# Three kinds of work at the end of a ConvFFN, moved one or two steps later

## The chip, the cores and the metric

The kernel runs on one core of a Trainium2 chip. The metric is the time of one launch in device microseconds. Before the change it is 2572.07 us, the median of three runs (2570.33 to 2573.21). The core has five engines that run side by side, each working through its own queue in order: TensorE (PE in the profile; its weight loads are PEld), VectorE (DVE), ScalarE (ACT), GpSimd (POOL) and SyncE (SP), which here only issues DMA transfers. Some transfers are issued from POOL's queue, those that add into DRAM.

## The reference

The program is a trunk of two layers over 1024 rows of width 1024 in float32: layer 0 has a gated DeltaNet and a ConvFFN, layer 1 a chunked attention and a ConvFFN, each with an RMSNorm ahead and a residual sum behind, and a final RMSNorm. The change concerns the ConvFFN, which both layers have, and what follows it in layer 0:

```python
def rmsnorm(x, g):
    xf = x.astype(jnp.float32)
    y = xf * lax.rsqrt(jnp.mean(xf * xf, axis=-1, keepdims=True) + EPS)
    return (y * g.astype(jnp.float32)).astype(x.dtype)

def conv_ffn(xn, w_up, conv_w, conv_b, w_down):
    h = causal_dwconv(xn @ w_up, conv_w) + conv_b          # 3 taps along the rows
    gate, val = h[..., :FFN_DIM], h[..., FFN_DIM:]         # FFN_DIM = 2816 = 22 tiles of 128
    return (jax.nn.silu(gate) * val) @ w_down
...
        h = h + conv_ffn(rmsnorm(h, f_norm[layer]), f_w_up[layer], f_conv[layer], f_conv_b[layer], f_w_down[layer])
```

## The kernel before

Every matrix product is done in float32 by three matmuls of rounded parts: an operand is rounded to `fp32r` (the high part, a copy on ScalarE), the rest is a difference (the low part, a subtraction on VectorE or GpSimd), and high by high, low by high and high by low are summed in PSUM. A "rounding" is that pair of instructions: `uh`/`ul` for the first weights, `dh`/`dl` and `eh`/`el` for the second product, `hidh`/`hidl` for hidden tiles, `fh`/`fl` for the last weights.

`ffn` (line 1423, called once for each layer) goes through 22 tiles j of 128 hidden channels. A tile has a gate half and a value half of 128 x 1024. The two products with the first weights are done by a scheme with seven block products instead of eight (`product`, in the order n = 1, 7, 6, 5, 2, 4, 3), whose banks are read and combined by `after`: ScalarE copies `keep` (n = 1) and half of `gpre` (n = 2); VectorE makes two `keep` sums (n = 6), the halves of `vpre` (n = 5 and 4) and the other half of `gpre` (n = 3). Product 4 adds into the bank of product 7, which the second `keep` sum reads first. Then a tile is convolved: `taps` (line 1544) makes step 0 on ScalarE (L1553) and steps 1 and 2 on VectorE (L1556), for value and gate; `silu` (L1559) is on ScalarE; `gated` (line 1561) multiplies value by gate on VectorE; `hidden` (line 1564) rounds the result. There is one buffer for `gate`.

The first 18 tiles go through a second scheme in pairs (`second`, `drain`, `send`), which ends in DMA sums into DRAM. The last four tiles, 18 to 21, are multiplied directly with the last rows of the second weights into banks `pf`: in layer 0 by `part` (eight output tiles m, three passes over them for the first 512 rows: tiles 18 and 19, then 20, then 21; then one pass for the other 512 rows), in layer 1 by `tile_of`, the same with eight row tiles. The last weights are loaded by `load_last`, and `cut_last` (line 1855) rounds them: q is the output tile in layer 0; the low part is VectorE's for even q and GpSimd's for odd q. Tile 21, the last, is convolved in halves of 512 rows: `half(c0, c1)` (line 1712) returns two functions, the first with the three value taps and the first two gate taps, the second with the last gate tap, `silu`, `gated` and `hidden`.

The order is written by hand. `step(key, f)` appends a step of matmuls to a list `seq` and notes its place in `pos`; `at(i, f, rank)` books other work ahead of step i. At the end one loop (line 1992 on) goes through the steps: for each it sorts the booked work by rank (equal ranks keep the order of booking), issues it, and then issues the step. All five engines get their instructions in that order:

```python
            for i in range(len(seq) + 8):
                for _, f in sorted(jobs.pop(i, ()), key=lambda j_: j_[0]):
                    f()
                if i < len(seq):
                    seq[i]()
```

`end` is the place of tile 21's last product (n = 3), `fin_at` that of the second scheme's last product; `nx(j, s)` is the place of product number s of the next tile, and for the last tile `end + s`. `pf` of output tile 0 is step `end + 1`, of output tile 1 `end + 2`, and so on.

Behind layer 0's `ffn` stands the norm of its result (`norm_steps`, line 391). `closing` (line 1884) adds `pf` to the residual `h` on VectorE, and with each `h` goes a square on ScalarE (`nacc` for the first, `nt` for the others, L399) and a sum on VectorE (L401); the last sum is L409. For the first 512 rows the column sums `pss` (L412) and the spread `psb` (L425) are matmuls among those of the second pass. While that runs, `load_w` and `split_w` (line 91) load and prepare the attention's first weights: a load into `wraw`, a fold with a norm's gains on ScalarE (L96, eight small instructions), `whi` on ScalarE (L102) and `wlo` on GpSimd (L104). This work is outside the hand-written list: its place among the norm's instructions on ScalarE and SP is chosen by the Tile framework's own ordering.

Of the kernel before, what the change touches and what calls it, by code (L numbers as in the profile page):

```python
# [19 lines left out]
HALF = 512  # L20
NH_A = 8
NH_B = 16
FP = 22
# [5 lines left out]
def trunk_kernel(  # L29
# [541 lines left out]
    with ExitStack() as ph:  # L571
# [140 lines left out]
        def heads(t):  # L712

            return t // 2, range(4 * (t % 2), 4 * (t % 2) + 4)
# [656 lines left out]
        with tc.manual_schedule(engines={mybir.EngineType.PE, mybir.EngineType.DVE, mybir.EngineType.Activation}):  # L1371
            tails = []
            acts, normed = [[[[None, None] for _ in range(KT)] for _ in range(2)] for _ in range(2)]
            for t in range(4):
                s, hds = heads(t)
# [47 lines left out]
    def ffn(layer, h, hp, xs, tail, d_r, last):  # L1423
# [19 lines left out]
        def at(i, f, rank=1):  # L1443

            jobs.setdefault(max(i, 0), []).append((rank, f))
# [98 lines left out]
        def taps(j, v, step, c0=0, c1=SEQ):  # L1544
            w, m = cf[:, layer, FP * v + j, :], FP * v + j
            if (j, v) not in conv_t:
                if v == 0:
                    conv_t[j, v] = tp.tile([P, SEQ], F32, name="gate", tag="gate")
                else:
                    conv_t[j, v] = hp.tile([P, SEQ], F32, name="val", tag=f"h{layer + 1}_{j % 4}")  # L1550
            t_, p_ = conv_t[j, v], pre[j, v]
            if step == 0:
                nc.scalar.activation(t_[:, c0:c1], p_[:, c0:c1], AF.Identity, scale=w[:, 2:3], bias=cfb[:, layer, m : m + 1])  # L1553
            else:
                a = max(c0, step)
                nc.vector.scalar_tensor_tensor(t_[:, a:c1], p_[:, a - step : c1 - step], w[:, 2 - step : 3 - step], t_[:, a:c1], op0=ALU.mult, op1=ALU.add)  # L1556

        def silu(j, c0=0, c1=SEQ):
            nc.scalar.activation(conv_t[j, 0][:, c0:c1], conv_t[j, 0][:, c0:c1], AF.Silu)  # L1559

        def gated(j, c0=0, c1=SEQ):
            tt(nc.vector, conv_t[j, 1][:, c0:c1], conv_t[j, 1][:, c0:c1], conv_t[j, 0][:, c0:c1], ALU.mult)

        def hidden(j, c0=0, c1=SEQ):

            if j not in hid:
                if j == FP - 1:
                    hid[j] = [fin.tile([P, SEQ], F32R, name=f"hid{i}", tag=f"hid{i}") for i in "hl"]
                else:
                    room_ = {18: (5, 6), 19: (7, 2), 20: (3, 4)}[j]  # L1570
                    hid[j] = [hp.tile([P, SEQ], F32R, name=f"hid{i}", tag=f"h{layer + 1}_{n}") for n, i in zip(room_, "hl")]
            (hh, hl), v_ = hid[j], conv_t[j, 1]
            nc.scalar.copy(hh[:, c0:c1], v_[:, c0:c1])
            tt(nc.vector, hl[:, c0:c1], v_[:, c0:c1], hh[:, c0:c1].bitcast(F32), sub)
# [29 lines left out]
        pos = {}  # L1604
# [42 lines left out]
        end, fin_at = pos[FP - 1, 7], pos["d", NG - 1, 4]  # L1647
# [15 lines left out]
        def nx(j, s):  # L1663
            return pos[j + 1, s] if j + 1 < FP else end + s
# [24 lines left out]
        for j in range(3, FP - 1):  # L1689
# [3 lines left out]
        v0, v1, v2, g0, g1, g2 = [(v, i) for v in (1, 0) for i in range(3)]  # L1693
        when = {
            0: [(11, (g0,), 0), (12, (v0,), 0), (13, (v1,), 2), (13, (v2,), 2.7), (15, (g1, g2, silu), 2), (17, (gated,), 2)],
            1: [(18, (v0, v1), 2), (19, (v2, g0), 2), (20, (g1,), 2), (21, (g2, silu), 2), (22, (gated,), 2)],
            2: [(24, (v0, v1), 2), (25, (v2, g0), 2), (26, (g1,), 2), (27, (g2, silu), 2), (28, (gated,), 2)],
        }
        for j in range(3, FP - 1):
            late_ = 1 if j == FP - 2 else 0  # L1700
            when[j] = [(pos[j, 7], (v0, v1), 2), (nx(j, 1), (v2, g0), 2), (nx(j, 2 + late_), (g1,), 2)]
            when[j] += [(nx(j, 3 + late_), (g2,), 2), (nx(j, 4 + late_), (silu,), 1.6), (nx(j, 5 + late_), (gated,), 2)]
            if j >= 2 * NG:
                when[j].append(({18: fin_at + 5, 19: pos[FP - 1, 5], 20: end + 1}[j], (hidden,), 1.9))
        for j, w_ in when.items():
            for i, fs, r in w_:
                at(i, lambda j=j, fs=fs: [taps(j, *f) if isinstance(f, tuple) else f(j) for f in fs], r)
# [4 lines left out]
        def half(c0, c1):  # L1712
            return (
                lambda: (taps(FP - 1, 1, 0, c0, c1), taps(FP - 1, 1, 1, c0, c1), taps(FP - 1, 1, 2, c0, c1), taps(FP - 1, 0, 0, c0, c1), taps(FP - 1, 0, 1, c0, c1)),
                lambda: (taps(FP - 1, 0, 2, c0, c1), silu(FP - 1, c0, c1), gated(FP - 1, c0, c1), hidden(FP - 1, c0, c1)),
            )
# [5 lines left out]

        fin = None
        at(end, open_fin, -2)
        at(end, half(0, HALF)[0], 2)
        at(end + 1, half(0, HALF)[1], 2)
        at(end + 2, lambda: (half(HALF, SEQ)[0](), half(HALF, SEQ)[1]()), 2)

# [108 lines left out]
        fw, fh, fps, norms = {}, {}, {}, []  # L1837
        n0 = len(seq)
        slots = [(k, 1) for k in range(4)] + [(k, 1) for k in range(4, 8)] if layer == 0 else [(k, 0) for k in range(4)] + [(k, 1) for k in range(4)]
        last_at = [pos[FP - 1, s] for s in (3, 4, 5, 6)] + ([end, end, end + 1, end + 1], [end + 1, end + 1, end + 3, end + 3])[layer]  # L1840

        def load_last(q):
            tag = ("a11", "a12", "r11", "r21", "r22", "r11", "r22", "r21")[q]
# [18 lines left out]
        for q in range(8):  # L1862
            s = (1, 1, 2, 3, 4, 4, 5, 6)[q]
# [143 lines left out]
    d_h = [dram.tile([P, SEQ], F32, name=f"d_h{k}") for k in range(KT)]  # L2007
    xb = ([[None, None] for _ in range(KT)], [[None, None] for _ in range(KT)])
    ctx_f, tail0 = ffn(0, h, hp, normed, tails[0], d_r0, xb)
    ctx_o = ctx.enter_context(ExitStack())  # L2010
    wp = ctx_o.enter_context(tc.tile_pool(name="wp1", bufs=2, **SB))
# [315 lines left out]
    def norm_out(t, ht, fin):  # L2327
# [34 lines left out]
        return go()  # L2362

    ctx_f, _ = ffn(1, h, hp, normed, tails[0], d_r1, norm_out)
    ctx_f.close()
    ctx_h.close()
# [56 lines left out]
```

## Time and profile before

| | before |
|---|---|
| median of the runs | 2572.07 us |
| profiled execution, its own time | 2572.95 us |
| its span | 2571.2 us |
| TensorE busy | 2504.6 us (97%) |
| VectorE, ScalarE, GpSimd busy | 72%, 55%, 57% |
| tile 21's products and `pf` in layer 0 | about 1260 to 1334 us of the span |
| the same in layer 1 | about 2492 to 2565 us |

The span is the time from the first to the last instruction in the profile; the execution's own time is 1.75 us longer. A row of a timeline has the start in the span, the duration, the engine, the line and operation, the tile written and the tiles read, and a count; in brackets stands how long the engine was idle before it and what ended that. Rows that follow each other without idle time and have the same line are merged. A window's row has the busy time of each engine (with the number of instructions), then the granted TensorE clock as a share of full speed, the DMA share and GB/s. A row of the waits has the total, the count and the longest, in microseconds. Most of the helper functions record under one line, so L1428 is every elementwise operation of `ffn` and L1449 every rounding's copy but those of `cut_last` (L1858) and `hidden` (L1573).

### The profile page before, as it was taken

To read this page: it belongs to the slowest core of one execution; us is meant where nothing else is said; L and a number is where in the kernel's file an instruction comes from. 1 tells how busy PE (TensorE), PEld (TensorE's weight loads), DVE (VectorE), ACT (ScalarE), POOL (GpSimd) and SP (SyncE) were. 2 spreads that over 40 slices of the span, in tenths; PEclk is the share of its full clock that TensorE was granted. 3 is DMA by queue.
4 is the path that set the end of the run, shared out by engine and by line. 5 is a ranking of instruction groups with operands and counts; after the bars stand their busy time and mean duration, and the time that the engine had idled before them with its cause. 6 is when DMAs were issued, how large, how long until landed. Compare 5 with 4: busy or idle time off the path is not lost.

```text
span 2571.2 us, 39377 instructions
## 1 busy us (share of the span) xinstructions
PE 2504.6 (97%) x13933; PEld 2070.5 (81%) x13933; DVE 1863.4 (72%) x3103; ACT 1417.1 (55%) x2736; POOL 1471.5 (57%) x1466
## 2 busy tenths in 40 slices
PE   7999999999999999999999999999999999999998
PEld 5878888888877888888778888887877788888877
DVE  5775874554688888888876666666488788888886
ACT  6444545474455556565546565555455655556554
POOL 3655553445347777777726444443433777777770
PEclk9999999999999999999999999999999999999999
DMA  4543445555337777777931211113332567677785
GB/s 127 137 110 114 127 124 152 156 170 161 95 86 149 144 154 153 154 144 152 203 120 54 65 52 56 44 51 101 91 111 78 135 142 152 142 153 157 150 188 203
DMA packets 320598, 325.15 MB, mean 126 GB/s; under 512 B 32912, under 2 KB 244624, under 8 KB 320400
## 3 DMA queue, kind: packets, MB, share of 16 engines
q1 hardware_dynamic: 289440, 219.33, 28.9%
q0 software_dynamic: 25920, 94.38, 20.6%
q10 hardware_dynamic: 5040, 8.91, 1.0%
q8 instruction: 110, 1.80, 0.3%
q14 instruction: 88, 0.72, 0.1%
HBM read 179.89 MB, written 142.67 MB: 125 GB/s over the span
## 4 chain that ended last, share of the span: by engine, by line
PE 54%; DVE 6%; issue 4%; POOL 3%; ACT 2%; DMA 1%; POOLq 0%; ACTq 0%; SPq 0%; DVEq 0%
PE pu L1463 8%; PE pu L1461 8%; PE pu L1462 8%; PE pd L1463 4%; PE pd L1461 4%; PE pd L1462 4%; PE acc L119 3%; PE acc L120 3%; PE acc L121 3%; POOL ul L1428 2%; PE ptp L2139 2%; PE sc L2111 1%; PE poT L2169 1%; PE poT L2168 1%; PE sc L2112 1%
## 5 line engine op out<-in xcount | busy, mean ns | idle before, releaser
L1428 POOL TENSOR_TENSOR ul<-r,uh 128x512 fp32r<-128x512 f32 x282 | 443.1, 1591 | 305.6 <-ACT uh L1449 290.0
L119 PE MATMUL acc<-xh,whi 128*128 128x512 f32 x896 | 373.0, 417 | 1.8 <-DVE kq L686 1.6
L120 PE MATMUL acc<-xl,whi 128*128 128x512 f32 x896 | 353.3, 394 | 1.6 <-POOL xl L421 1.0
L121 PE MATMUL acc<-xh,wlo 128*128 128x512 f32 x896 | 352.4, 393 | 1.1 <-POOL wlo L104 1.1
L1449 ACT CAST uh<-r 128x512 fp32r<-128x512 f32 x296 | 181.9, 623 | 221.2 <-DVE r L1428 166.8
L104 POOL TENSOR_TENSOR wlo<-wraw,whi 128x256 fp32r<-128x256 f32 (+2 forms) x206 | 170.2, 856 | 148.6 <-ACT whi L102 139.2
L1461 PE MATMUL pu<-xh,uh 128*128 128x512 f32 x552 | 215.4, 390 | 1.5 <-DVE h L1329 0.9
L1463 PE MATMUL pu<-xh,ul 128*128 128x512 f32 x552 | 215.4, 390 | 1.1 <-POOL ul L1428 1.0
L1462 PE MATMUL pu<-xl,uh 128*128 128x512 f32 x552 | 215.1, 390 | 1.0 <-POOL xl L421 1.0
L1786 ACT COPY stage<-pd 128x1024 f32<-128x1024 f32 x180 | 175.1, 1014 | 49.4 <-PE pd L1463 45.7
L121 PEld LDWEIGHTS acc<-xh,wlo 128*128 128x128 f32 x896 | 168.6, 188 | 38.8 <-POOL wlo L104 1.6
L120 PEld LDWEIGHTS acc<-xl,whi 128*128 128x128 f32 x896 | 169.9, 190 | 26.1 <-POOL xl L421 3.1
L119 PEld LDWEIGHTS acc<-xh,whi 128*128 128x128 f32 x896 | 169.5, 189 | 24.3 <-DVE kq L686 2.0
L2119 POOL TENSOR_SCALAR sS<-sS,st 128x640 f32<-128x640 f32 (+4 forms) x128 | 85.6, 671 | 170.3 <-DVE st L2118 120.1
L1556 DVE SCALAR_TENSOR_TENSOR val<-vpre,colt,val 128x1023 f32<-128x1023 f32 (+2 forms) x92 | 150.6, 1637 | 41.4 <-ACT val L1553 41.2
L1428 POOL TENSOR_TENSOR dl<-a,dh 128x512 fp32r<-128x512 f32 x90 | 154.8, 1720 | 38.5 <-ACT dh L1449 37.2
L1556 DVE SCALAR_TENSOR_TENSOR gate<-gpre,colt,gate 128x1023 f32<-128x1023 f32 (+2 forms) x92 | 175.9, 1912 | 0.8
L1428 DVE TENSOR_TENSOR r<-r,r 128x512 f32<-128x512 f32 x168 | 132.9, 791 | 29.4 <-POOL ul L1428 28.1
L2117 ACT ACTIVATE sS<-sS,st 128x640 f32<-128x640 f32 (+4 forms) x128 | 89.3, 697 | 101.0 <-DVE st L2116 97.6
L1463 PEld LDWEIGHTS pu<-xh,ul 128*128 128x128 f32 x552 | 103.6, 188 | 24.6 <-POOL ul L1428 3.2
L1461 PEld LDWEIGHTS pu<-xh,uh 128*128 128x128 f32 x552 | 103.6, 188 | 23.5 <-issue 1.3
L1462 PEld LDWEIGHTS pu<-xl,uh 128*128 128x128 f32 x552 | 103.6, 188 | 23.3 <-POOL xl L421 2.0
(405 smaller groups left out, 7158.4 us busy)
## 6 DMA issues: line engine op xcount, KB each, us to landing
r<-in_f_w_up_dram SPq DMA_DIRECT2D x176, 256.0 KB, 4.4
d_r<-stage POOLq DMA_DIRECT2D x78, 512.0 KB, 7.8
d_c<-stage POOLq DMA_DIRECT2D x70, 512.0 KB, 7.9
a<-in_f_w_down_dram SPq DMA_DIRECT2D x72, 256.0 KB, 2.9
wraw<-in_a_w_in_dram SPq DMA_DIRECT2D x32, 512.0 KB, 4.5
d_e<-stage POOLq DMA_DIRECT2D x32, 512.0 KB, 8.9
wraw<-in_a_w_out_dram SPq DMA_DIRECT2D x16, 512.0 KB, 4.4
d_r<-h ACTq DMA_DIRECT2D x32, 256.0 KB, 3.8
```

Of the source, the lines that this page charges most:

```text
L104: nc.gpsimd.tensor_tensor(lo[:, c], raw[:, c], hi[:, c].bitcast(F32), op=ALU.subtract)
L119: mm(ps, hi[:, kw, wcol : wcol + P], rh[k][s], start=st, stop=False)
L120: mm(ps, hi[:, kw, wcol : wcol + P], rl[k][s], start=False, stop=False)
L121: mm(ps, lo[:, kw, wcol : wcol + P], rh[k][s], start=False, stop=sp)
L1428: tt = lambda eng, o, a, b, op: eng.tensor_tensor(o, a, b, op=op)
L1449: copy(hi, src)
L1461: mm(ps, w[0][:, cw], x[0], start=first, stop=False, skip_group_check=True)
L1462: mm(ps, w[0][:, cw], x[1], start=False, stop=False, skip_group_check=True)
L1463: mm(ps, w[1][:, cw], x[0], start=False, stop=last, skip_group_check=True)
L1556: nc.vector.scalar_tensor_tensor(t_[:, a:c1], p_[:, a - step : c1 - step], w[:, 2 - step : 3 - step], t_[:, a:c1], op0=ALU.mult, op1=ALU.add)
L1786: nc.scalar.copy(t_, ps)
L2117: nc.scalar.activation(S, S, AF.Exp, bias=st[:, 1:2], accum_out=st[:, 2:3])
```

## The change

Four bookings move; no computing instruction or transfer is added or removed.

```diff
@@ for j in range(3, FP - 1)
             late_ = 1 if j == FP - 2 else 0
             when[j] = [(pos[j, 7], (v0, v1), 2), (nx(j, 1), (v2, g0), 2), (nx(j, 2 + late_), (g1,), 2)]
-            when[j] += [(nx(j, 3 + late_), (g2,), 2), (nx(j, 4 + late_), (silu,), 1.6), (nx(j, 5 + late_), (gated,), 2)]
+            when[j] += [(nx(j, 3 + late_), (g2,), 2), (nx(j, 4 + late_), (silu,), 1.6), (end + 1 if late_ else nx(j, 5), (gated,), 1.8 if late_ else 2)]
             if j >= 2 * NG:
-                when[j].append(({18: fin_at + 5, 19: pos[FP - 1, 5], 20: end + 1}[j], (hidden,), 1.9))
+                when[j].append(({18: fin_at + 5, 19: pos[FP - 1, 5], 20: end + 2}[j], (hidden,), 1.9))
...
         at(end, open_fin, -2)
-        at(end, half(0, HALF)[0], 2)
+        at(end + 1, half(0, HALF)[0], 2)
         at(end + 1, half(0, HALF)[1], 2)
...
-        last_at = [pos[FP - 1, s] for s in (3, 4, 5, 6)] + ([end, end, end + 1, end + 1], [end + 1, end + 1, end + 3, end + 3])[layer]
+        last_at = ([pos[FP - 1, s] for s in (5, 6, 7, 7)] + [end + 1, end + 1, end + 2, end + 2], [pos[FP - 1, s] for s in (3, 4, 5, 6)] + [end + 1, end + 1, end + 3, end + 3])[layer]
```

In both layers the gate product of tile 20 goes from the fifth product of tile 21 to `end + 1`, its rounding (`hidden`) from `end + 1` to `end + 2`, and the first part of tile 21's first half from `end` to `end + 1`, directly ahead of its second part. In layer 0 alone the roundings of the last weights 0 to 7 move: 0 and 1 by two steps, 2 by two, 3 by one, 4 to 7 by one each; layer 1 keeps its places.

VectorE's queue at layer 0's end, before and after (`val20` is the product for tile 20, `/a` and `/b` the first and second 512 rows):

```
before: hidl18, val tap2 (20), fl0, gate tap1 (20), keep, keep, r12, gate tap2 (20), vpre, fl2, hidl19, val20,
        vpre, fl4, val taps 1, 2 (21/a), gate tap1 (21/a), gpre, fl6, hidl20, gate tap2 (21/a), val21/a, hidl21/a, half b
after:  hidl18, val tap2 (20), gate tap1 (20), keep, keep, r12, gate tap2 (20), vpre, fl0, hidl19,
        vpre, fl2, gpre, fl4, val20, val taps 1, 2 (21/a), gate tap1 (21/a), gate tap2 (21/a), val21/a, hidl21/a, fl6, hidl20, half b
```

On ScalarE `fh0` moves behind two roundings of first weights, `fh1` and `fh2` behind its copy into `gpre`, and `fh6`, `fh7` and `hidh20` behind `silu` and `hidh` of tile 21's first half. On GpSimd `fl1` moves behind two `ul`. TensorE's order is the same in all of the kernel. In layer 1 VectorE has `gpre`, `fl4`, `val20` ahead of tile 21's taps, and `hidl20` behind `hidl21/a`.

Outside `ffn`, the Tile framework orders three queues differently at the seam to the attention. On ScalarE the first square `nacc` of the norm stands ahead of the eight L96 of the first weights (before: behind them), and the L96 are spread among the following squares; the second `whi` stands behind the first square of the second 512 rows (before: ahead of two squares of the first 512). On SP the third load of `wraw` stands behind seven stores of `h` instead of three, the fourth behind three stores of the second half. GpSimd's order is unchanged there.

## The prediction

> **What bounds the kernel now.** I read the page first (busy shares, the chain that ended last), then TensorE's table of waits, then the three engines' timelines over the two places where the diff acts, and last the windows for the clock.
>
> ```profile
> PE 2504.6 (97%) x13933; PEld 2070.5 (81%) x13933; DVE 1863.4 (72%) x3103; ACT 1417.1 (55%) x2736; POOL 1471.5 (57%) x1466
> PE pu L1461 <- DVE keep L1428: 2.5, 2, 1.6
> ```
>
> TensorE is busy 97% of the span, so a reordering gains only what TensorE waits or runs slowly. The waits at the ends of the two FFNs are small. Those for `keep` are two, 2.5 us together, one in each layer. Layer 0's end in TensorE's timeline (start, duration, and in brackets the idle time before it and what ended that):
>
> ```profile
> 1267.78 0.39 PE L1463 MATMUL pu<-xt2h,ul 128*128 128x512 f32 x1
> 1274.55 0.47 PE L1461 MATMUL pu<-xt4h,uh 128*128 128x512 f32 x1 [0.94 <-DVE keep L1428]
> 1280.07 0.39 PE L1461 MATMUL pf<-hidh,fh 128*128 128x512 f32 x1
> 1281.43 0.39 PE L1461 MATMUL pf<-hidh,fh 128*128 128x512 f32 x1
> 1286.28 0.47 PE L1461 MATMUL pf<-hidh,fh 128*128 128x512 f32 x1 [1.96 <-DVE gpre L1428]
> 1293.18 0.39 PE L1461 MATMUL pf<-hidh,fh 128*128 128x512 f32 x1
> 1315.68 0.50 PE L1461 MATMUL pf<-hidh,fh 128*128 128x512 f32 x1 [0.58 <-DVE h L1428]
> 1321.67 1.39 PE L412 MATMUL pss<-ones,nacc 128*128 128x2 f32 x8 [1.58 <-DVE nacc L409]
> 1328.46 0.75 PE L1461 MATMUL pf<-hidh,fh 128*128 128x512 f32 x1
> ```
>
> Each of the eight output tiles `pf` starts with six matmuls in 1.36 us (1280.07 to 1281.43). The third step (tile 20) of tile 0 starts at 1293.18. Between lie 8 x 1.36 = 10.9 us of work and the 1.96 wait.
>
> **Part 1, tile 0's rounding `fl0` leaves its place.** Why `keep` was late:
>
> ```profile
> 1266.17 1.73 DVE L1428 TENSOR_TENSOR fl<-fr,fh 128x512 fp32r<-128x512 f32 x1
> 1267.82 5.25 DVE L1556 SCALAR_TENSOR_TENSOR gate<-gpre,colt,gate 128x1023 f32<-128x1023 f32 x1
> 1274.92 1.27 DVE L1556 SCALAR_TENSOR_TENSOR gate<-gpre,colt,gate 128x1022 f32<-128x1022 f32 x1
> 1265.71 1.64 POOL L1428 TENSOR_TENSOR ul<-r,uh 128x512 fp32r<-128x512 f32 x1 [0.98 <-ACT uh L1449]
> 1267.92 1.59 POOL L1428 TENSOR_TENSOR ul<-r,uh 128x512 fp32r<-128x512 f32 x1
> 1269.18 1.56 POOL L1428 TENSOR_TENSOR fl<-fr,fh 128x512 fp32r<-128x512 f32 x1
> 1270.43 1.56 POOL L1428 TENSOR_TENSOR ul<-r,uh 128x512 fp32r<-128x512 f32 x1
> ```
>
> A gate tap takes 1.27 us alone, and 5.25 here: it ends 1.1 us after GpSimd's run of three (1271.99). In the new order `fl0` and GpSimd's `fl1` are gone from here. The tap stands where `fl0` stood and waits as that did for the `ul` that ends at 1267.35, so it ends near 1268.5; `keep`, whose product in TensorE ends at 1268.2 (1267.78 + 0.39), follows in two sums by 1269.9. TensorE wants it at 1274.55 - 0.94 = 1273.6, a cover of 3.7 us. **Gain 0.94.** Next late is nothing: `ul` for tile 21's last product moves earlier with its DVE sum.
>
> **Part 2, the first taps, the gate product of tile 20 and tile 20's `hidl` move behind `gpre`.** What stood ahead of `gpre`, and what must now come after:
>
> ```profile
> 1278.26 1.23 DVE L1428 TENSOR_TENSOR hidl<-val,hidh 128x1024 fp32r<-128x1024 f32 x1 [0.36 <-ACT hidh L1573]
> 1279.40 2.32 DVE L1428 TENSOR_TENSOR val<-val,gate 128x1024 f32<-128x1024 f32 x1
> 1282.24 1.18 DVE L1428 TENSOR_TENSOR fl<-fr,fh 128x512 fp32r<-128x512 f32 x1
> 1283.34 1.52 DVE L1556 SCALAR_TENSOR_TENSOR val<-vpre,colt,val 128x511 f32<-128x511 f32 x2
> 1285.44 0.69 DVE L1428 TENSOR_TENSOR gpre<-pu,keep 128x512 f32<-128x512 f32 x1
> 1279.31 3.56 POOL L1428 TENSOR_TENSOR fl<-fr,fh 128x512 fp32r<-128x512 f32 x2 [1.96 <-ACT fh L1858]
> 1278.60 1.66 ACT L1858 CAST fh<-fr 128x512 fp32r<-128x512 f32 x3
> 1289.10 0.63 ACT L1559 ACTIVATE gate<-gate 128x512 f32<-128x512 f32 x1 [3.25 <-DVE gate L1556]
> 1290.49 0.62 ACT L1573 CAST hidh<-val 128x512 fp32r<-128x512 f32 x1 [0.76 <-DVE val L1428]
> ```
>
> The fourth `pf` tile waited for the bank that `gpre` reads. New order on VectorE: `vpre`, `fl2`, `gpre`, `fl4`, the product, three taps, a tap, product, `hidl` of 21's first half, `fl6`, `hidl` of 20. With part 1, `hidl` of tile 19 ends near 1276.1, the last product of 21 near 1279.2, so `gpre` lies at 1279.2 to 1279.8 (with GpSimd's run in the way, it ends at 1280.8). TensorE, 0.94 earlier than before, starts `pf` at 1279.1 and wants the fourth bank at 1279.1 + 3 x 1.36 = 1283.2. **Gain 1.96.**
>
> The price: `fh6`, `fh7` on ScalarE and `fl6` on VectorE now stand behind a chain that alternates engines. From `gpre`'s end: `fl4` to 1280.8, product 1.2 to 1282.0, two value taps 1.45 and a gate tap 0.7 to 1284.15, a gate tap 0.65 to 1284.8, silu 0.63, product 0.69, `hidh` 0.62 to 1286.8, `hidl` to 1287.5, `fl6` to 1288.1; `fh6` follows `hidh`, 1287.4. A wait is added: the one `gate` buffer makes ScalarE's first gate tap of tile 21 wait for the product of tile 20 (1282.0 instead of `gpre`, 1279.8); behind it queue silu, `hidh`, `fh6` and `fh7`, but the two value taps on VectorE cover it. TensorE starts tile 6 at 1279.1 + 6 x 1.36 = 1287.3 and needs `fl6` at 1287.7. That is 0.45 late; 1.05 if GpSimd's three roundings `fl1`, `fl3`, `fl5` hold VectorE up as in part 1. Bounds: 0 (all in time) and 2.9 (two more products blocked by one GpSimd rounding of 1.25 each). I take **0.7**, between 0.45 and 1.05, since the rows show both manners. `hidl` of tile 20 comes at 1290.3, needed at 1290.9 behind the wait, so it is covered by 0.6; tile 21's second half (1296) by 5 us. SP's loads into the freed rounding buffers go up to 1 us earlier, and GpSimd's DMA issues keep their order.
>
> On the blocking, the row comes first: the 5.25 tap let three GpSimd instructions pass, while the 2.32 product got in between two (1279.31, x2). [...]
>
> **Part 3, the seam behind layer 0.** Tile's ordering of ScalarE changes there: `nacc` and the first squares now come ahead of most of the fold of the next weights (`wraw`, L96), and the second `whi` (with GpSimd's `wlo` behind it) after the second half's first square.
>
> ```profile
> 1299.48 2.46 ACT L96 ACTIVATE wraw<-wraw,colt 128x128 f32<-128x128 f32 x8 [2.58 <-DMA wraw<-in_w_kv_dram]
> 1303.96 2.46 DVE L401 TENSOR_TENSOR nacc<-nacc,nt 128x512 f32<-128x512 f32 x1 [2.41 <-ACT nt L399]
> 1312.55 2.47 DVE L401 TENSOR_TENSOR nacc<-nacc,nt 128x512 f32<-128x512 f32 x1 [0.18 <-ACT nt L399]
> 1314.94 1.87 DVE L1428 TENSOR_TENSOR h<-pf,h 128x512 f32<-128x512 f32 x3
> 1320.52 1.09 DVE L409 TENSOR_TENSOR nacc<-nacc,nt 128x512 f32<-128x512 f32 x1
> 1312.07 2.40 POOL L104 TENSOR_TENSOR wlo<-wraw,whi 128x1024 fp32r<-128x1024 f32 x1 [6.19 <-ACT whi L102]
> ```
>
> ScalarE's 2.46 of folding ahead of `nt` makes VectorE idle 2.41, then a `wlo` (2.40) stretches a sum to 2.47, so `h` is read at 1314.94 though its bank was full seven microseconds before. With `nacc` and `nt` ahead, and TensorE 0.94 + 1.96 - 0.7 = 2.2 us earlier (first `h` at 1297), VectorE does the half's eight `h` and seven sums of 0.6 and one `wlo` stop of 2.4 by 1297 + 9 + 2.4 = 1308.4. The bank is needed at 1315.68 - 0.58 - 2.2 = 1312.9: **gain 0.58**, bounds 0 and 0.58. The final sum L409 must still follow the fifth tile of the second half, `h` 0.6, two sums 0.6 and 0.7, signals 0.2, less the 1.36 of matmuls queued ahead: a wait of 0.8 in place of 1.58, if no GpSimd work stands on the sums. By ScalarE's new order `nacc` 0.6, a fold 0.3, `nt` 0.6 and the cast 1.0 follow 1308.8, so the second `wlo` is at 1311.3 to 1313.7; the sums are at 1316.8 to 1318. **Gain 0.8**; bounds 0.8 and a loss of 1.8 (one sum blocked as at 1312.55, 2.47 for 0.68). The new `wraw` load on SP moves behind four more stores of `h`; its user, ScalarE's L336, has 30 us until the weights are used.
>
> The low clock behind that wait:
>
> ```profile
> 1320.00:1325.00 5.00, 3.42 (x14) 2.95 (x14) 1.82 (x3) 1.88 (x3) 2.08 (x3) 0.72 0.19 73
> 1902.57 1.05 PE L412 MATMUL pss<-ones,nacc 128*128 128x2 f32 x8 [1.35 <-DVE nacc L409]
> 1906.48 0.49 PE L1461 MATMUL pu<-xh,uh 128*128 128x512 f32 x1
> 1903.00:1906.00 3.00, 3.00 (x19) 2.60 (x18) 0.20 (x1) 0.74 (x2) 0.64 (x1) 1.00 0.66 184
> ```
>
> After 1.58 us of idling the granted clock fell to 0.72 as the mean of 1320 to 1325 (third figure from the end of the window's row); after 1.35 us before the same `pss` in layer 1 it stayed at 1.00. The same stretch (pss, nine matmuls, psb) took 1328.46 - 1321.67 = 6.79 here and 1906.48 - 1902.57 = 3.91 there. At a wait of 0.8 I expect the full clock: **gain 2.9**; bounds 0 and 2.9.
>
> **Part 4, layer 1's end.** Its roundings keep their steps.
>
> ```profile
> 2507.66 0.47 PE L1461 MATMUL pu<-xt4h,uh 128*128 128x512 f32 x1 [1.60 <-DVE keep L1428]
> 2520.14 1.21 DVE L1428 TENSOR_TENSOR hidl<-val,hidh 128x1024 fp32r<-128x1024 f32 x1
> 2527.87 0.39 PE L1957 MATMUL pf<-fh,hidh 128*128 128x512 f32 x1
> ```
>
> The 1.60 wait lies ahead of all that moves: it stays. `hidl` of tile 20 slides from 2520.1 to about 2522 and is used at 2527.9. **0**, with 5 us of cover; a loss only if the slide passed that.
>
> **Sum.** -0.94 - 1.96 + 0.7 - 0.58 - 0.8 - 2.9 = -6.5 us. The profiled execution took 2572.95, so 2566.5; the median of the runs is 0.9 lower, 2572.07, so 2565.6. I give 2566. No change can be told below 0.2%, 5.1 us: faster means under 2566.9.
>
> **Rivals.**
> *The clock still falls* (0.25). Whether it does depends on how idle and thin matmuls fall together: 1.35 kept it, 1.58 lost it. Then -3.6: 2568.5. [...]
>
> *The roundings come too late* (0.16). The chain behind `gpre` runs into GpSimd twice more, tile 6 waits 2.9, and parts 1 and 2 cancel. For it speaks the 2.32 product, against it that `gpre`, where the chain begins, itself comes 5 us earlier. The seam may still gain its 0 to 2: 2571.
>
> *The second `wlo` meets the final sum* (0.09), the slower side. If ScalarE's cast ends after 1314.4 instead of 1311.3, GpSimd's 2.40 stands on L401 or L409 as at 1312.55; the wait is 1.58 + 2.4 and the low clock lasts once more (2.9). -2.2 - 0.58 + 2.4 + 2.9 = +2.5: 2574.6. Against it stand those 3.1 us of margin.
>
> **How the numbers follow.** My forecast has 0.5; its own range is 2564.2 to 2567.6. The full range, 2563.5 to 2572.5, leaves out the slower rival and a little of the upper side. Faster by 5.1: four fifths of the forecast and little else, 0.41. Slower by 5.1 needs the slower rival and more: 0.04. Same: 0.55.
>
> **What would show it.** No `keep` wait in layer 0, no `gpre` wait; tile 6 of `pf` waiting under 1 us for ScalarE or VectorE; third step begun 2.2 us earlier relative to 1273.2; no `h` wait; `pss` waiting about 0.8 with the clock at 1.00 behind it; the 1.60 wait of layer 1 unchanged. Wrong if `fh6` waits over 2 us, if the clock still falls behind `pss`, or if waits of the attention that follows, which all starts earlier, shift by several microseconds.

## The result and the profile after

The changed kernel takes 2566.54 us (median of 13 runs, 2562.51 to 2569.00), the kernel before, in as many runs beside it, 2571.82 us (2569.33 to 2574.36): a ratio of 0.9979 with a 95% interval of 0.9972 to 0.9986, 5.3 us or 0.21% faster. 2566.0 was predicted. The profiled execution took 2567.06 us, its span 2565.4.

The page's busy shares of the changed kernel, and its two rows for the waits that the prediction spoke of (total, times, longest):

```profile
PE 2502.9 (98%) x13933; PEld 2070.2 (81%) x13933; DVE 1856.2 (72%) x3103; ACT 1416.0 (55%) x2736; POOL 1468.9 (57%) x1466
PE pu L1461 <- DVE keep L1428: 1.6, 1, 1.6
PE pss L412 <- DVE nacc L409: 2.6, 3, 1.4
```

The wait for `gpre` is gone from the table and that for `keep` is there once, in layer 1. TensorE's timeline over layer 0's end, at the places that the prediction showed of before, and layer 1's `keep` as the last row:

```profile
1268.11 0.39 PE L1463 MATMUL pu<-xt2h,ul 128*128 128x512 f32 x1
1273.77 0.39 PE L1461 MATMUL pu<-xt4h,uh 128*128 128x512 f32 x1
1283.29 0.39 PE L1461 MATMUL pf<-hidh,fh 128*128 128x512 f32 x1
1287.65 0.50 PE L1461 MATMUL pf<-hidh,fh 128*128 128x512 f32 x1
1288.46 0.50 PE L1463 MATMUL pf<-hidh,fl 128*128 128x512 f32 x1
1290.85 0.39 PE L1461 MATMUL pf<-hidh,fh 128*128 128x512 f32 x1
1312.61 0.39 PE L1461 MATMUL pf<-hidh,fh 128*128 128x512 f32 x1
1317.48 1.05 PE L412 MATMUL pss<-ones,nacc 128*128 128x2 f32 x8 [0.63 <-DVE nacc L409]
1321.39 0.49 PE L1461 MATMUL pf<-hidh,fh 128*128 128x512 f32 x1
2501.81 0.47 PE L1461 MATMUL pu<-xt4h,uh 128*128 128x512 f32 x1 [1.58 <-DVE keep L1428]
```

From the first of these matmuls to the last but one the same work takes 1321.39 - 1268.11 = 53.28 us; before it took 1328.46 - 1267.78 = 60.68. I call this the stretch; it is compared for every kernel below. Subtracting the starts row by row against the rows of before gives its 7.40 us: 1.11 at `keep`, 2.21 at the fourth `pf` tile, 0.66 lost at tile 6, 0.74 at the `h` wait, 1.12 at `pss`, 2.88 in the nine matmuls behind it. (Each wait that goes saves some 0.2 more than its idle time. Matmuls in sequence start 0.23 us apart and last 0.39, so idle time, which is counted from the end of the matmul before, leaves out 0.16; and the matmul behind a wait ran longer, 0.47 for 0.39.)

VectorE in the changed kernel, from the tap that was blocked to tile 6's rounding, and GpSimd's last roundings:

```profile
1266.44 2.31 DVE L1556 SCALAR_TENSOR_TENSOR gate<-gpre,colt,gate 128x1023 f32<-128x1023 f32 x1
1268.67 1.40 DVE L1428 TENSOR_TENSOR keep<-pu,keep 128x512 f32<-128x512 f32 x2
1279.41 0.69 DVE L1428 TENSOR_TENSOR gpre<-pu,keep 128x512 f32<-128x512 f32 x1 [1.43 <-PE pu L1463]
1280.86 1.21 DVE L1428 TENSOR_TENSOR val<-val,gate 128x1024 f32<-128x1024 f32 x1
1287.71 0.69 DVE L1428 TENSOR_TENSOR fl<-fr,fh 128x512 fp32r<-128x512 f32 x1
1276.01 4.37 POOL L1428 TENSOR_TENSOR fl<-fr,fh 128x512 fp32r<-128x512 f32 x3 [1.95 <-ACT fh L1858]
1316.74 0.69 DVE L409 TENSOR_TENSOR nacc<-nacc,nt 128x512 f32<-128x512 f32 x1
```

`keep` ends at 1270.1 (forecast 1269.9), `gpre` at 1280.1 (1279.8), `fl6` at 1288.4 (1288.1); VectorE now idles 1.43 us ahead of `gpre` for TensorE, where TensorE had idled for it. The final sum L409 takes 0.69 instead of 1.09.

Not all of the 7.40 arrives at the end. The profiled execution is only 5.9 us shorter (2572.95 - 2567.06): the `pss` of layer 1 (1895 us) now has a low clock behind it, which it had not before. The two windows, each 3.41 us, show the stall and what follows (third figure from the end: granted clock):

```profile
1892.73:1896.15 3.42, 2.05 (x14) 1.51 (x13) 2.27 (x2) 0.88 (x2) 2.98 (x2) 1.00 0.09 35
1896.15:1899.56 3.41, 3.41 (x10) 2.74 (x10) 0.20 (x1) 0.74 (x2) 0.16 (x1) 0.50 0.82 231
```

Followed matmul by matmul, the gain on before falls there by 1.55 us. The experiments had to settle three things: which part of the change removes which wait, what decides over the clock (the length of a stall or its phase, that is, where it lies against the windows of 3.41 us in which the trace shows the clock low), and what layer 1's `keep` hangs on.

### The profile page after: what moved, and what is told of

Same layout as the page of the kernel before. It is cut to its first block, busy times and chain, and to the rows that moved or that the text cites. A ratio compares the mean times of both kernels' runs of the same rounds, so it can differ in the third digit from the quotient of the medians.

```text
span 2565.4 us, 39382 instructions
## 1 busy us (share of the span) xinstructions
PE 2502.9 (98%) x13933; PEld 2070.2 (81%) x13933; DVE 1856.2 (72%) x3103; ACT 1416.0 (55%) x2736; POOL 1468.9 (57%) x1466
## 4 chain that ended last, share of the span: by engine, by line
PE 55%; DVE 6%; POOL 4%; issue 3%; ACT 2%; DMA 0%; ACTq 0%; POOLq 0%; DVEq 0%
PE pu L1463 8%; PE pu L1462 8%; PE pu L1461 8%; PE pd L1463 4%; PE pd L1461 4%; PE pd L1462 4%; PE acc L119 3%; PE acc L120 3%; PE acc L121 3%; POOL ul L1428 2%; PE ptp L2139 2%; PE poT L2169 1%; PE sc L2111 1%; PE poT L2168 1%; PE sc L2112 1%
```

## The experiments

One number per kernel recurs, the stretch; the medians stand beside it. The changed kernel's own runs lie up to 6.5 us apart and its two medians 1.2, and in the profiles the clock falls at other places too, not the same ones in each. So the verdicts rest on the stretch, though it is that of one profile each, and the clock has a part in it that is named where it matters.

| kernel | stretch, us | median, us | kernel before, beside it | ratio, 95% interval |
|---|---|---|---|---|
| before; a second profile | 60.68; 58.40 | | | |
| after; a second profile | 53.28; 53.28 | 2566.54; 2565.35 | 2571.82; 2572.03 | 0.9972 to 0.9986; 0.9969 to 0.9987 |
| roundings alone | 56.36 | 2567.64 | 2571.23 | 0.9980 to 0.9998 |
| taps alone | 55.01 | 2566.99 | 2571.23 | 0.9979 to 0.9996 |
| folds late | 57.53 | 2566.85 | 2571.23 | 0.9977 to 0.9995 |
| roundings and folds | 54.08 | 2566.47 | 2570.50 | 0.9976 to 0.9993 |
| first four roundings and folds | 56.64 | 2568.77 | 2570.50 | 0.9983 to 1.0000 |
| after, longer wait | 55.78 | 2566.71 | 2571.23 | 0.9975 to 0.9992 |
| after, six early | 53.34 | 2565.02 | 2572.03 | 0.9963 to 0.9981 |
| after, layer 1 late; again | 53.28; 53.25 | 2564.32; 2564.32 | 2572.03; 2570.50 | 0.9964 to 0.9983; 0.9969 to 0.9987 |
| after, both | 53.37 | 2564.05 | 2572.03 | 0.9960 to 0.9983 |

**Roundings alone.** The kernel before with one line of the change:

```diff
-        last_at = [pos[FP - 1, s] for s in (3, 4, 5, 6)] + ([end, end, end + 1, end + 1], [end + 1, end + 1, end + 3, end + 3])[layer]
+        last_at = ([pos[FP - 1, s] for s in (5, 6, 7, 7)] + [end + 1, end + 1, end + 2, end + 2], [pos[FP - 1, s] for s in (3, 4, 5, 6)] + [end + 1, end + 1, end + 3, end + 3])[layer]
```

> The kernel before, with only the eight roundings of layer 0's last weights one or two steps later. Both theories have the keep wait of layer 0 (0.94) gone, since the 5.25 us gate tap no longer meets GpSimd's run of three. Theory A, the prediction's (each part pays for its own wait): the gpre wait of 1.96 stays, because the two taps, the gate product and hidl still stand ahead of gpre. Theory B (one cause): the 5.25 us tap held up VectorE's whole queue by 3.6 to 4 us, so gpre, which ended at 1286.1, now ends near 1282 and is wanted at 1283.2: the gpre wait goes too, and moving the taps is worth nothing by itself. ScalarE's order at the seam stays as before, nine folds ahead of the first square: if that order is what keeps h late, the h wait grows from 0.58 by most of what TensorE has gained and the pss wait stays above 1.5 us; if h was late only through VectorE's end of the FFN, the 0.58 stays or shrinks. Time against the kernel before: A about -1, B about -3 if the seam lets the gain through, 0 to -1 if the seam takes it back.

Its VectorE rows at the tap and at `gpre`, and TensorE's at tile 6 and `pss`:

```profile
1267.14 2.31 DVE L1556 SCALAR_TENSOR_TENSOR gate<-gpre,colt,gate 128x1023 f32<-128x1023 f32 x1
1282.85 0.68 DVE L1428 TENSOR_TENSOR gpre<-pu,keep 128x512 f32<-128x512 f32 x1
1289.11 0.50 PE L1461 MATMUL pf<-hidh,fh 128*128 128x512 f32 x1 [0.86 <-ACT fh L1858]
1319.73 1.05 PE L412 MATMUL pss<-ones,nacc 128*128 128x2 f32 x8 [1.40 <-DVE nacc L409]
```

Theory B holds. With nothing moved ahead of `gpre`, its wait is gone all the same: the tap takes 2.31 instead of 5.25, the queue behind it runs earlier, and `gpre` ends at 1283.5, before TensorE's fourth bank (1284.0). Tile 6 pays more than in the changed kernel, 1.42 us instead of 0.66, as `fh6` stands behind the whole chain with the product and `hidl` of tile 20 still in it. The `h` wait is gone as well, although nine folds still stand ahead of the first square on ScalarE: that order is not what kept `h` late. The seam keeps a `pss` wait of 1.40 and one low window.

**Taps alone.** The other three lines of the change, without the roundings.

> The kernel before, with only the first taps, tile 20's gate product and its hidl moved, in both layers. Theory A: the keep wait of 0.94 stays, the gpre wait of 1.96 goes, and tile 6 of pf does not wait, because fh6 and fh7 still stand ahead of the silu chain. Theory B: the same FFN numbers; the two theories differ only in that by B this part gains nothing on top of the roundings, by A it gains its 1.96 in either company. At the seam three folds stand ahead of the first square instead of nine: h wait under 0.6, pss wait between 0.6 and 1.6. Time against the kernel before: -2 where the clock behind pss still falls, -5 where it does not.

```profile
1277.95 0.47 PE L1461 MATMUL pu<-xt4h,uh 128*128 128x512 f32 x1 [0.92 <-DVE keep L1428]
1295.80 0.50 PE L1462 MATMUL pf<-hidl,fh 128*128 128x512 f32 x1 [0.77 <-DVE hidl L1428]
1322.34 1.05 PE L412 MATMUL pss<-ones,nacc 128*128 128x2 f32 x8 [0.63 <-DVE nacc L409]
```

`keep` waits 0.92 and `gpre` not at all, as expected of both theories. So each part alone removes the `gpre` wait; the prediction had given it to part 2 only. Not expected was the 0.77 for `hidl` of tile 20: the prediction had it covered by 0.6 in the changed kernel, where tile 6 delays TensorE by 0.66; here nothing delays it, and the cover is gone.

**Folds late.** FFN untouched; ScalarE's fold of the next weights is queued behind squares of the norm, about where the changed kernel has it:

```diff
-            nc.scalar.activation(sq, h[k][:, hs(s)], AF.Square)
+            env["sq", g is None, s, k] = nc.scalar.activation(sq, h[k][:, hs(s)], AF.Square).ins
...
-    first = two_tiles([load_w(w_kv, 0, fold=g_kv, on_act=True), load_w(b_w_q, 0, fold=g_b, on_act=True)], tail0)
+    with tc.issue_after(env["sq", True, 0, 1]):
+        wt0 = load_w(w_kv, 0, fold=g_kv, on_act=True)
+    with tc.issue_after(env["sq", True, 0, 7]):
+        wt1 = load_w(b_w_q, 0, fold=g_b, on_act=True)
+    first = two_tiles([wt0, wt1], tail0)
```

> The kernel before with its FFN untouched, and only ScalarE's folds of the next weights queued behind the second and the last square of the first norm half: the seam's order alone. Theory A (the seam's part is a matter of ScalarE's order): the h wait of 0.58 goes, the pss wait falls from 1.58 to 0.6 to 0.9, the clock behind it stays at 1.00 and the nine matmuls win their 2.9: -4.2 at the end of the seam, with keep 0.94 and gpre 1.96 unchanged. Rival (the seam gained only because TensorE's FFN ended earlier or because the phase of the clock's window changed): h and pss waits within 0.3 of before, or the waits shorter and the clock still low, 0 to -1.4.

```profile
1286.12 0.47 PE L1461 MATMUL pf<-hidh,fh 128*128 128x512 f32 x1 [1.93 <-DVE gpre L1428]
1321.27 1.05 PE L412 MATMUL pss<-ones,nacc 128*128 128x2 f32 x8 [0.63 <-DVE nacc L409]
1320.53 0.69 DVE L409 TENSOR_TENSOR nacc<-nacc,nt 128x512 f32<-128x512 f32 x1
1286.00:1296.00 10.00, 9.88 (x36) 8.01 (x37) 7.76 (x10) 3.31 (x5) 0.50 (x1) 0.83 0.34 124
```

The `pss` wait falls to the changed kernel's 0.63 with the FFN as before, so this part of the seam is a matter of ScalarE's order and not of when the FFN ends. (The `h` wait is gone too, but TensorE comes there 1.6 us later, behind the low clock, so of `h` this run says nothing.) The mechanism differs from the one that the prediction priced: the last sums, L401 and L409, take 0.68 and 0.69 here and in the changed kernel. In before L409 took 1.09, and the timelines of its VectorE and GpSimd have

```profile
1319.52 1.07 DVE L401 TENSOR_TENSOR nacc<-nacc,nt 128x512 f32<-128x512 f32 x1
1318.84 3.25 POOL L338 TENSOR_TENSOR wraw<-wraw,colt 128x256 f32<-128x256 f32 x4 [4.36 <-DMA wraw<-in_w_kv_dram]
```

so GpSimd's L338 ran beside both. That is 0.8 of the 0.95. In the two other profiles in which L338 runs beside the last two sums it is the whole excess over 0.63: with the roundings alone the sums take 1.04 and 1.10, 0.77 more, for a wait of 1.40; in the second profile of before 1.14 and 1.10, 0.87 more, for 1.50. L338 hangs on ScalarE's order by a chain: the load that it waits for is issued when the second `wlo` has read the buffer (at 1314.50 in before, where that `wlo` ends at 1314.47), and the `wlo` follows the second `whi`. With the folds late this `wlo` ends at 1318.31 and L338 starts at 1323.12, behind the sums. From the third step (1293.18 in before) on, the kernel gains 4.8 us. But the clock fell at another place, behind `gpre` (0.83 over 1286 to 1296), where before had kept it, and the stretch is only 3.15 shorter.

**Longer wait.** The changed kernel with the `pss` wait brought back by other means:

```diff
+            if g is None and s == 0:
+                for _ in range(2):
+                    nc.vector.tensor_scalar(before, before, 1.0, None, op0=ALU.mult)
             nc.vector.tensor_tensor(acc, acc, before, op=ALU.add)
```

> The changed kernel with two more VectorE instructions of about 0.5 us each (a multiplication by one) ahead of the last sum of layer 0's first norm half, so that pss waits about 1.6 instead of 0.63. If the length of the wait decides over the clock: the granted clock falls behind this pss as before and the stretch of nine matmuls takes 2.9 longer, +4 in all against the changed kernel. If it is a matter of phase: the wait grows by 1 and the clock may well stay at 1.00, +1, and other stalls of the run show a fall where the changed kernel's profile had none.

Its lines are numbered three higher behind the insertion.

```profile
1319.13 1.05 PE L415 MATMUL pss<-ones,nacc 128*128 128x2 f32 x8 [1.55 <-DVE nacc L412]
1317.00:1330.00 13.00, 11.45 (x52) 9.48 (x51) 7.24 (x14) 4.67 (x7) 2.75 (x5) 0.87 0.32 112
```

The wait of 1.55 is back, and so is a low clock, but a shorter one: the stretch grows by 2.50, 0.93 of it the wait and 1.55 the nine matmuls, where before had lost 2.88 in them. Neither theory had that size. The length of the wait plays a part, and something else does too.

**Both kernels a second time.** Nothing edited.

> The changed kernel once more, nothing edited, for a second profile. If the clock behind a stall is a matter of phase, a second execution shows it low behind other stalls than the first (which had it low at 549, 1895 and 1950 us and full at 723, 1317 and 1759), while every wait stays within 0.1 us. If the length of the stall decides, the same stalls show it low. Layer 1's keep wait: 1.58 again if it belongs to the order of the kernel; another value, from 0 to 1.6, if it hangs on which of VectorE and GpSimd starts first within some 0.3 us, as the runs with 0, 0.78 and 0.94 suggest. Time about 2566.5.

> The kernel before once more, nothing edited, for a second profile. The waits that belong to its order repeat within 0.1 us: keep 0.94 and gpre 1.96 in layer 0, h 0.58, pss 1.58. If a pss wait of about 1.5 always loses the clock, the nine matmuls behind it take 1.2 to 2.9 longer again; if it is a matter of phase alone, they may run at 1.00. Layer 1's keep wait lies between 0 and 1.6. Time 2571 to 2572.

The changed kernel repeats its stretch to 0.01 us and loses the clock at the same stalls. Taken alone that speaks for the length of the stalls; but the times of its falls lie only 0.43 us from those of the first profile, counted from the start of the stretch, so it hardly tried another phase. The kernel before does not: its second profile has the same waits for `keep` (0.94), `gpre` (1.97) and `pss` (1.50), yet the clock falls behind `gpre` and not behind `pss`, the other way round than in the first. Windows of 3.41 us around both stalls, first profile of before:

```profile
1284.67:1288.08 3.41, 1.80 (x8) 1.54 (x9) 3.41 (x5) 1.18 (x2) 1.68 (x1) 1.00 1.05 393
1318.81:1322.22 3.41, 1.83 (x11) 1.29 (x10) 2.80 (x4) 1.98 (x3) 3.25 (x4) 1.00 0.65 248
1322.22:1325.63 3.41, 3.41 (x12) 2.83 (x12) 0.20 (x1) 0.27 (x1) 0.00 (x0) 0.50 0.00 0
1325.63:1329.05 3.42, 3.42 (x14) 3.03 (x13) 1.42 (x3) 0.63 (x1) 0.00 (x0) 0.50 0.23 81
```

and its second profile:

```profile
1283.97:1287.38 3.41, 1.44 (x7) 0.98 (x6) 3.38 (x6) 1.85 (x3) 1.69 (x1) 1.00 1.06 397
1287.38:1290.79 3.41, 3.41 (x10) 2.63 (x9) 2.29 (x3) 0.96 (x2) 0.00 (x0) 0.50 0.59 216
1318.10:1321.51 3.41, 2.66 (x12) 1.88 (x10) 2.88 (x5) 2.05 (x4) 2.73 (x4) 1.00 0.83 315
1321.51:1324.92 3.41, 2.66 (x16) 2.36 (x17) 0.97 (x3) 0.92 (x2) 0.14 (x1) 1.00 0.05 17
```

The windows are not chosen at will. In steps of 0.1 us the granted clock is seen to fall in one step from 1.00 to 0.50 and to return after 3.41 or 6.83 us; in the first profile it falls at 550.81, 1322.22, 1759.13 and 1957.10, and these lie 226, 128 and 58 steps of 3.4133 us apart, to 0.02 us (the step is the one that fits them). In every other profile too the falls lie whole such steps apart. So in these profiles the falls keep to a grid that runs through the execution, and the stalls lie on it as they happen to. First profile: a grid line at 1284.67 cuts the `gpre` wait (1284.32 to 1286.28) into 0.35 and 1.61, no fall; the whole `pss` wait lies in one window with a part of the thin `pss` matmuls, fall. Second profile: the whole `gpre` wait of 1.97 lies in one window, fall; a line at 1321.51 cuts the `pss` wait into 0.75 and 0.75, no fall. Of the full-clock windows without `pss` in all fourteen profiles, leaving out the first 20 us, the 544 to 560 us with their 32x32 and 64x64 matmuls and what reaches past the last matmul, those that idled 1.75 us or more were followed by a low window and those that idled 1.70 or less were not (at 1.73 both happened, one at 1.74 was not followed). (One window at the very end, with the folds late, idled 1.89 without a fall behind it.) Where all of a `pss` lies in the window, 1.05 us or more of 128x2 matmuls, falls came after less idling: from 1.04 us on, none up to 0.90. No run shows why. Nor does one show why the first profile of before has a second low window; its first one held the rest of `pss`. A low window cost 1.5 to 1.6 us (1.55 at layer 1's `pss`), the two in a row of the first profile 2.88.

The windows ahead of these two falls were not idle throughout: TensorE was busy for 1.83 us of the one ahead of the first profile's fall and for 1.44 of the one ahead of the second's.

By these counts I estimate that the 0.63 wait does not lose the clock in any phase, unless other idle time falls in the same window: it lies under 0.90, and 0.63 and all of the 1.05 us of `pss` come to 1.68, under the 1.75. It kept it in all ten profiles that had it. The `pss` of layer 1 with 1.34 to 1.38 went either way: low behind it in seven of the fourteen, among them both of the changed kernel and the second of before.

**Six early.** `last_at` of the changed kernel for layer 0 with `end + 1` for tiles 6 and 7:

```diff
-  ... + [end + 1, end + 1, end + 2, end + 2], ...
+  ... + [end + 1, end + 1, end + 1, end + 1], ...
```

> The changed kernel with the last two of layer 0's roundings (tile 6 and 7) one step earlier, so that they stand ahead of the taps of tile 21 again. If they wait only behind the silu chain, the 0.52 at tile 6 (0.27 for fh, 0.25 for fl) goes, and nothing takes its place: -0.5 against the changed kernel. If they now push that chain back, hidl of tile 20 is late instead (it was covered by 0.6 us in the prediction; with the taps moved alone it was late by 0.77): 0 to +0.7.

```profile
1291.23 0.50 PE L1462 MATMUL pf<-hidl,fh 128*128 128x512 f32 x1 [0.56 <-DVE hidl L1428]
```

Tile 6 does not wait, and `hidl` of tile 20 does, 0.56. The stretch is 53.34 instead of 53.28: the second expectation, a zero sum. Both hang on the same chain behind `gpre`.

**Layer 1 late,** and **both**, which joins it to the edit above. The changed kernel with layer 1's first four roundings where layer 0's are:

```diff
-  ..., [pos[FP - 1, s] for s in (3, 4, 5, 6)] + [end + 1, end + 1, end + 3, end + 3])[layer]
+  ..., [pos[FP - 1, s] for s in (5, 6, 7, 7)] + [end + 1, end + 1, end + 3, end + 3])[layer]
```

> The changed kernel with the first four roundings of layer 1's last weights put at the steps that layer 0's have now. If the roundings on VectorE and GpSimd ahead of the gate tap make the wait for keep in layer 1, it goes in every execution: -1.6 against one with the wait, 0 against one without. If the tap meets the two ul of GpSimd anyway, up to 1 us of it stays. What could be late instead: fh and fl of the first tiles at layer 1's end, with fewer steps ahead of their use, 0 to +1.

> The changed kernel with layer 1's first four roundings later, a second time, on one chip with the other candidate: no keep wait in layer 1, the median 0.5 to 1.5 below the changed kernel's, 2564 to 2565.

> The changed kernel with both of the edits: tile 6 and 7 of layer 0 a step earlier, and layer 1's first four roundings as late as layer 0's. By the theory that each wait is its own, -0.5 and 0 to -1.6: about -1.5 against the changed kernel, 2565. By the rival that the displaced work is late elsewhere, 0 to +1.7.

In all of them layer 1's `keep` does not wait, and nothing late takes its place (matmul by matmul they gain 1.8 us there on the first profile of before). Across the other profiles this wait, in a layer that most of them leave alone, was anything: 1.60 and 1.11 (before), 1.58 and 0.94 (after), 1.60 with the roundings alone, 0.94 with the taps alone, 0.78 with the folds late, 0.74 with six early, 0.42 with roundings and folds, and next to none (0.15) with the longer wait. The rows say what it hangs on. With the taps alone, VectorE's tap and GpSimd:

```profile
2499.03 5.26 DVE L1556 SCALAR_TENSOR_TENSOR gate<-gpre,colt,gate 128x1023 f32<-128x1023 f32 x1
2499.12 2.84 POOL L1428 TENSOR_TENSOR ul<-r,uh 128x512 fp32r<-128x512 f32 x2
2501.63 1.57 POOL L1428 TENSOR_TENSOR fl<-fr,fh 128x512 fp32r<-128x512 f32 x1
```

and with the folds late, the same code in layer 1 but for the order around it:

```profile
2497.83 2.31 DVE L1556 SCALAR_TENSOR_TENSOR gate<-gpre,colt,gate 128x1023 f32<-128x1023 f32 x1
2496.07 2.99 POOL L1428 TENSOR_TENSOR ul<-r,uh 128x512 fp32r<-128x512 f32 x2 [0.68 <-PE pu L1463]
2499.02 2.26 POOL L1428 TENSOR_TENSOR fl<-fr,fh 128x512 fp32r<-128x512 f32 x1
```

The tap that begins with the run of three takes 5.26 us and ends at 2504.29, behind all of the run, which ends at 2503.20 (though the tap's record starts 0.09 ahead of it; so did before's 5.25 tap in layer 0, 1267.82 against a GpSimd `ul` at 1267.92). The tap that begins 1.76 us into the run takes 2.31 and ends at 2500.14, 1.08 behind the second `ul` (2499.06), and then GpSimd's `fl` is the longer one (2.26 for 1.57). Why all three instructions end ahead of the tap in one case and two in the other is open.

The longest of these waits, 1.58 to 1.60, has the same source one instruction earlier. In the changed kernel's first profile the run ends at 2498.59, ahead of VectorE's rounding `fl0`, which began 0.21 behind the run's start and ends at 2499.14; the tap behind it, at 2499.07, takes 1.27:

```profile
2494.72 4.42 DVE L1428 TENSOR_TENSOR fl<-fr,fh 128x512 fp32r<-128x512 f32 x1 [1.92 <-ACT fh L1858]
2494.51 2.83 POOL L1428 TENSOR_TENSOR ul<-r,uh 128x512 fp32r<-128x512 f32 x2
2497.02 1.57 POOL L1428 TENSOR_TENSOR fl<-fr,fh 128x512 fp32r<-128x512 f32 x1
```

In the first profile of before this `fl0` took 5.06, with the roundings alone 4.00. What helped in both layers was to take `fl0` from its place ahead of the tap and `fl1` out of the run; no experiment moved only one of the two.

The medians of layer 1 late, 2564.32 twice, lie below the changed kernel's 2565.35, measured beside the first of them; the intervals of the ratios overlap, so the times do not tell them apart, and the gain of up to 1.6 us stands on the traces.

**Roundings and folds; first four roundings and folds.** The kernel before with the folds late, and with the roundings of layer 0 as in the change, or with only the first four later, in both layers:

```diff
-        last_at = [pos[FP - 1, s] for s in (3, 4, 5, 6)] + ([end, end, end + 1, end + 1], [end + 1, end + 1, end + 3, end + 3])[layer]
+        last_at = [pos[FP - 1, s] for s in (5, 6, 7, 7)] + ([end, end, end + 1, end + 1], [end + 1, end + 1, end + 3, end + 3])[layer]
```

> The kernel before with layer 0's eight roundings later and the folds of the next weights queued behind the squares, the taps left where they were. The two parts were -1.9 (FFN, roundings alone) and -5.05 (seam, folds alone) from 1273 to 1330 us; if they add up, -6.9, with pss waiting 0.63 and the clock full behind it: 2565. The moved taps would then be worth the 0.7 that the changed kernel has more in the FFN. If the seam needs the moved taps, or a later end of the FFN, h and pss wait longer and less than 4 of the 5.05 comes.

> The kernel before with only the first four roundings of the last weights later, in both layers (tiles 4 to 7 keep their steps), and the folds queued behind the squares; the taps stay. If the run of roundings beside the gate tap is the one cause in each layer, the keep and gpre waits of layer 0 (0.94 and 1.96) go, tile 6 does not wait, since its roundings stand where they stood, and layer 1's keep wait goes: -2.9, -5.05 and -0 to -1.6 against before, 2562.5 to 2564, one to two below the changed kernel. If fl2 and the fl of tiles 4 and 5, now closer together ahead of gpre, hold it up, up to 1.9 of gpre's wait stays and it is level with the changed kernel.

Roundings and folds add up: the roundings alone gained 1.89 up to the third step, the folds alone 4.78 from there on, 6.67 together, and 60.68 - 54.08 = 6.60 came, with `pss` waiting 0.62. What the moved taps add to that is 0.80 (54.08 against 53.28), the cheaper tile 6. The median, 4.0 below before's, shows less of it; in its profile the clock is low at five places outside the stretch, in before's two at three and at two.

Four roundings alone fail where the other expectation had it. `keep` does not wait, in either layer, but `gpre` does:

```profile
1282.02 2.88 DVE L1428 TENSOR_TENSOR fl<-fr,fh 128x512 fp32r<-128x512 f32 x2
1287.97 0.68 DVE L1428 TENSOR_TENSOR gpre<-pu,keep 128x512 f32<-128x512 f32 x1
1279.08 5.27 POOL L1428 TENSOR_TENSOR fl<-fr,fh 128x512 fp32r<-128x512 f32 x3 [1.95 <-ACT fh L1858]
1288.80 0.57 PE L1461 MATMUL pf<-hidh,fh 128*128 128x512 f32 x1 [2.28 <-DVE gpre L1428]
```

The four roundings moved on to the four that stayed: two `fl` on VectorE and a run of three on GpSimd ahead of `gpre`, and it waits 2.28, longer than before. What stands ahead of `gpre` counts as much as the tap.

## Why the prediction was right, and where it was not

- **Part 1, `keep`, 0.94:** right, 1.11 counted from row to row. The tap ends 1.09 behind one `ul` (1268.75 against 1267.66), 2.31 in all, as forecast; the cover of 3.7 us was ample. But the reach was drawn too short: the tap's 5.25 had pushed back all of VectorE's queue, `gpre` with it.
- **Part 2, `gpre`, 1.96:** right in size (2.21) and in the place of `gpre` to 0.3 us. Wrong in cause: the roundings alone remove it, and so do the taps alone. The two terms were not two causes; in the sum this did no harm, because the change makes both moves.
- **The price, 0.7 (0.45 to 1.05):** 0.66, of which 0.27 us is tile 6's `fh` and 0.25 its `fl`. The chain behind `gpre` came as timed (`fh6` 1287.6 against 1287.4). The rival of late roundings did not occur. The cover of 0.6 for `hidl` was real and small: in three of the experiments it was gone, 0.77 and twice 0.56.
- **`h`, 0.58:** gone, 0.74, but not for the reason given. With the roundings alone it is gone too, with ScalarE's folds still ahead of the squares and two sums stretched to 2.46 and 2.47 by `wlo`. It was a thin wait: it is also missing from before's second profile, where TensorE came 1.6 us later.
- **`pss`, 0.8 of 1.58 left:** 0.63. The reason was half right: ScalarE's order decides, but 0.8 of the 0.95 is that GpSimd's L338 no longer runs beside the last two sums. Those rows (1.09 for L409, 0.69 for the same sum at other places) were quoted and not read for it. The rival of the second `wlo` did not occur: in the changed kernel its GpSimd row ends at 1313.9, three microseconds ahead of L409.
- **The clock, 2.9:** 2.88, and against before's first profile it was the largest term. Its step, "at a wait of 0.8 I expect the full clock", held in every profile; that 1.58 loses it and 1.35 keeps it did not, since before's second profile keeps it at 1.50 and the changed kernel loses it at 1.37. The rival, that it hangs on how idle time and thin matmuls fall together, was the true description of before, not of after: it is before that loses 1.6 to 2.9 behind one stall or the other, by where they lie on the grid, and of the two stalls the change leaves none at `gpre` and 0.63 at `pss`, behind which no profile had a low clock. Against before's second profile the stretch gains 58.40 - 53.28 = 5.1, against the first 7.4.
- **Part 4, 0, "the 1.60 wait of layer 1 stays":** it stayed at 1.58 in the profile and was 0.94 in the next. It is not a fixed wait, but in the matmuls behind it the moves in layer 1 cost nothing, as forecast.
- **Left out:** the later stalls. The sum let everything behind the seam arrive unchanged; layer 1's `pss` took back 1.55 in this pair of profiles. The prediction named only that such waits might shift. With it -7.4 becomes -5.9. That the forecast of 2566.0 landed 0.5 us from the median is in part luck: the stretch was underrated by 0.9 (0.6 of it the time that idle times leave out at `keep`, `gpre` and `h`, 0.3 at `pss`), and an unforeseen fall of the clock took that back and more.

## What to carry to other kernels

Before two terms are added, ask whether one of them is the cause of the other: a single blocked instruction near the head of a queue can delay what stands behind it (here `gpre` ended at 1286.1 behind the tap of 5.25, at 1283.5 with the roundings alone, behind the same tap in 2.31), and an experiment with each part alone tells it. Where TensorE's clock moves, compare stretches of equal work in two profiles of the same kernel before a low clock is put down to the edit; here falls came from about 1.75 us of idle time in a window of 3.41, and from 1.04 where all of a `pss` with its thin matmuls lay in it, and a stall of 0.63 kept the clock in all ten profiles that had it. And roundings or other filler that are moved pile up on what stays: check the run that they form on an engine that holds up the critical queue; here VectorE's taps and roundings that lay beside GpSimd's runs of three took up to 5.26 us (a tap of 1.27) and 5.06 (a rounding).

## What was not expected of the hardware

- In all fourteen profiles the granted clock fell on a grid of 3.4133 us and, up to the last matmul, stayed at 0.50 for whole steps, mostly one (up to three near 550 us); outside the stretches and the one window named above, a step without `pss` that idled 1.75 us or more was followed by a low one. With all of a `pss` in the step, no profile shows what happens between 0.90 and 1.04 us of idling.
- A VectorE tap of 1.27 us took 5.26 when it began together with a run of three GpSimd instructions, 2.31 when it began inside one; a start 1.85 us later against the run (1.76 into it for 0.09 ahead of it) went with 2.95 us less. Nor does a start inside the run always help: two VectorE roundings that began 0.2 and 0.5 us into its first instruction took 4.42 and 4.00, and in the folds-late profile one that began 0.5 us into it took 1.38.
- Beside GpSimd's fold L338 two VectorE sums took 0.4 us longer each (1.07 and 1.09 for 0.68 and 0.69), and TensorE's wait for the last was 1.58; the other sums of that stretch, beside no GpSimd work, took 0.68 or 0.69.
